# Scores of two levels in one visit of the recurrent branch, larger offsets in the order, and an earlier start of that branch

## The chip, the cores and the metric

The kernel runs on one core of one Trainium2 chip. The metric is the device time of one execution in microseconds (us). Three executions of the kernel before took 2306.87, 2311.93 and 2312.58 us; the median is 2311.93 us.

## What is computed

Two transformer blocks in float32, one after the other, on 512 tokens of width 1024. The change touches the first block alone, apart from one helper that both use. The first block normalizes `x`, projects it, and feeds three branches of 512 columns each, which are merged under gates:

```python
y_a = chunked_relpos_attention(a_q, a_k, a_v, rel_bias[l])      # branch a: attention with a bias by distance
y_b = hgrn2_recurrence(b_q, b_f, b_i, b_g, lb_all[l], ...)      # branch b: the recurrence
y_c = mla_attention(c_q, c_kv, c_kr, positions, ...)            # branch c: latent attention
up = einsum('bsnw,nwd->bsnd', stack([y_a, y_b, y_c]), w_branch[l])
merged = sum(sigmoid(gate_logits) * up, axis=2)
x = x + merged @ w_out[l]
x = x + square(relu(rmsnorm(x) @ w_ff1[l])) @ w_ff2[l]
```

The recurrence of branch b, for each of 8 heads of 64 columns, is

```python
k = (1 - lb) * sigmoid(-z);  q = silu(q)
cum = cumsum(log_f)                       # along the tokens
scores[i, j] = sum_d q[i,d] * k[j,d] * exp(cum[i,d] - cum[j,d])   # j <= i
o = scores @ v                            # plus a state carried from chunk to chunk
o = rmsnorm(o) * silu(g)
```

The second block has two layers, each with two kinds of attention (one of them a retention whose output is normalized per head), a convolutional feed-forward part and a gated addition.

## The kernel before, in words

**Matmuls.** Tiles are feature-major: 128 features by 512 tokens. A float32 product is made as three matmuls of a high and a low part (`lin`, L503: high weight by high x, low weight by high x, high weight by low x), each 128x128 by 512 columns. The weights come from memory in raw tiles of 512 KB, and ScalarE makes the high part (`wh`) and VectorE the low part (`wl`) of each.

**The order.** All instructions of an engine run in the order in which the program issues them, and that order is made by a planner inside the kernel. Every piece of work is a generator (a process) with a priority number. A process yields either nothing, a delay, an event or a condition; `drive` (L301) always continues the ready process with the lowest number. The planner keeps a time of its own, `now`, which only matmuls advance (`mm`, L378, by an estimate for each), and an estimate of when VectorE, ScalarE and GpSimd will have finished what has been issued to them (`Eng`, L211). `self.w("dv")` is the estimated time until VectorE is through, plus 200 ns. So a delay in a `yield` doesn't make any engine wait by itself: it moves what the process issues next behind more matmuls of others. If an estimate is too short, TensorE comes to the instruction before its operand is there, and waits.

**The stream.** One process of the lowest precedence, `stream` (L340), runs a list of tasks one after another: projections of 24 matmuls each (`proj`), the value projection of a branch (`values`, 96 matmuls of `v` into four PSUM banks), and `up` (24 matmuls, two output tiles of a branch's merge). `build` (L905) writes this list. `merge(n, m, ...)` (L1132) is two tasks `gate` and one `up`, so 72 matmuls. `bpair(pr)` is three projections (q, z, g), 72 matmuls, and starts the process `hgrn` of a pair of heads with priority 10 + pr. All of these processes come ahead of the stream wherever they are ready; the stream fills TensorE in between. After branch b's pairs and the merges of branch c come eight `gate` tasks, and then `up(1, m)`, which reads the four outputs of branch b, `yb`.

**One pair of branch b** (`hgrn`, L1254). The decayed scores are made level by level: at level s = 1, 2, 4, ..., 256 a query in the second half of a block of 2s tokens meets keys in its first half. `hlev` (L1352) makes for each level `eq` (ScalarE's exp of the running sum `pre`, then VectorE's product with q in `hmul`) and `ek` (exp of `suf`), and steps `pre` and `suf` to the next level with two VectorE additions. It keeps at most two levels in a list `fifo`. `hgrn` takes the first level of the list when its event has come (400 ns after the estimated end of the product), issues its score matmuls for the two heads into two PSUM banks (`level`, L1400, for s up to 64; inline for s of 128 and 256), and VectorE copies the banks through a mask into the two tiles `dg` (COPY_PREDICATED), or, for the two largest levels, `rsplit` splits them. Levels "0" and 1 go another way: `near` (L1388) transposes a product tile `t` on TensorE and sums it. After the last level come the products with the values (`pv`), the output `y`, and its norm (`gnorm`, L1201): squares, transposes (`gs`), a power and a broadcast on GpSimd (`rt`, `ex`), and transposes back (`pb`), after `yield self.w("gp")`. The split of the product is `yb[pr]`. `gnorm` is also used by the eight pairs of retention heads of the second block.

**Counters.** PSUM has eight banks, counted by `live["ps"]`; besides that each use has a limit of its own (`take`): score banks `sc` at most 3, projections `lin` at most 5, `po` 1. Two pairs of branch b can be under way at once.

Of the kernel before, what the change touches and what calls it, by code (L numbers as in the profile page):

```python
# [40 lines left out]
NT = S // 128  # L41
# [206 lines left out]
class Net:  # L248
# [656 lines left out]
    def build(self):  # L905
        I = self.I
        self.lincap = 5
        self.endp = None
        self.N = N = Norm()
        self.spawn(self.load_x(N), 1)  # L910
        self.spawn(self.rstd(N), 1)
        self.macc = [None] * KT
        self.gl = {}
        self.mx = [X() for _ in range(KT)]
        ya, yb, yc = ([X() for _ in range(4)] for _ in range(3))
        C = self.branch_c(N, yc)
        self.branch_a(N, ya, C)
        if self.stop == "a":
            return self.dump(ya)
        C.pair(0)  # L920
        self.gates(0, TUNE["GA"] + TUNE["GB"], N)
        C.pair(1)
        self.gates(0, TUNE["GA"] + TUNE["GB"] + TUNE["GC"], N)
        self.merge(0, 0, ya, N)
        C.pair(2)
        self.merge(0, 2, ya, N)
        C.pair(3)
        self.merge(0, 4, ya, N)
        self.merge(0, 6, ya, N)
        if self.stop == "c":  # L930
            return self.dump(yc)
        bpair = self.branch_b(N, yb)
        bpair(0)
        self.merge(2, 0, yc, N)
        bpair(1)
        self.merge(2, 2, yc, N)
        bpair(2)
        bpair(3)
        self.merge(2, 4, yc, N)
        self.merge(2, 6, yc, N)  # L940
        gs = [X() for _ in range(KT)]
        for m in range(KT):
            self.gate(1, m, N, gs[m])
        self.call(lambda: self.nfree(N))
        if self.stop == "b":
            return self.dump(yb)
        for m in range(0, KT, 2):
            self.up(1, m, yb, gs[m:m + 2], last=True)
        self.call(lambda: self.free(N.rb))
        self.x = [None] * KT  # L950
        N2 = Norm()
        self.wout1(N2)
        if self.stop == "mix":
            return self.dump(self.x)
        self.ffn1(N2)
# [245 lines left out]
    def gnorm(self, o, eps):  # L1201

        nc = self.nc
        sq = yield from self.g("sq")
        self.ac.activation(sq, o, AF.Square)
        yield self.w("ac")
        ps = yield from self.psr("po", 1, "gs")
        sums = yield from self.rowsum(ps, sq, HD)
        self.free(sq)
        ms = self.powm(sums, 2 * NT, 1.0 / HD, eps)  # L1210
        yield next(ms)
        self.free(ps)
        rt = yield from ms
        ex = yield from self.g("ex")
        self.pl.tensor_scalar(out=ex.rearrange("p (a b) -> p a b", b=64),
                                in0=rt.rearrange("p (a b) -> p a b", b=1).to_broadcast([128, 2 * NT, 64]),
                                scalar1=1.0, scalar2=1.0, op0=ALU.mult, op1=ALU.mult)
        yield self.w("gp")
        pb = yield from self.psr("po", 1, "pb")
        for t in range(NT):  # L1220
            s = slice(128 * t, 128 * t + 128)
            self.tr(pb[:, s], ex[:, s])
        self.free(ex)
        yield 300.0
        return pb
# [28 lines left out]
    def hgrn(self, pr, q, z, gz, vs, y):  # L1254
        nc = self.nc
# [17 lines left out]
        dg = []  # L1273
        for e in range(2):
            d = yield from self.g("dg")
            self.pl.memset(d, 0.0)
            dg.append(d)
        hi, lo = [], []
        fifo = []
        self.spawn(self.hlev(q, pre, suf, fifo), 1)  # L1280
        done = [Ev() for _ in range(2)]
        t = yield from self.g("t0")
        self.dv.tensor_tensor(out=t, in0=q, in1=k, op=ALU.mult)
        yield from self.near(t, 7, dg)
        cnt = [[0], [0]]
        s = 1
        while s < S:
            yield lambda: len(fifo) > 0
            eq, ek, ev = fifo[0]
            yield ev  # L1290
            if s == 1:
                t = yield from self.g("t1")
                self.pl.memset(t, 0.0)
                yield self.w("gp")
                tk, qq, kk = (x.rearrange("p (b u) -> p b u", u=2) for x in (t, eq, k))
                self.dv.tensor_tensor(out=tk[:, :, 0], in0=qq[:, :, 1], in1=kk[:, :, 0], op=ALU.mult)
                yield from self.near(t, 6, dg)
            elif s <= 64:
                yield from self.level(eq, ek, 6 - s.bit_length() + 1, dg)
                if s == 64:  # L1300
                    yield from self.take("Bt", 1, 1)
                    for e in range(2):
                        hi.append((yield from self.tri("sh", F32R)))
                        lo.append((yield from self.tri("sl", F32R)))
                    for e in range(2):
                        self.spawn(self.dsplit(dg[e], hi[e], lo[e], cnt[e], done[e]), 0)
            else:
                for e in range(2):
                    r = slice(64 * e, 64 * e + 64)
                    ps = yield from self.psr("sc", 3, "sc")  # L1310
                    if s == 128:
                        for c in range(2):
                            a, b = slice(256 * c, 256 * c + 128), slice(256 * c + 128, 256 * c + 256)
                            self.mm(ps[:, 128 * c:128 * c + 128], ek[r, a], eq[r, b], True, True)
                        arg = (128, 896, 128)
                    else:
                        for c in range(2):
                            self.mm(ps[:, 256 * c:256 * c + 256], ek[r, 128 * c:128 * c + 128], eq[r, 256:512], True, True)
                        arg = (256, 384, 256)
                    self.spawn(self.rsplit(ps, hi[e], lo[e], arg, cnt[e], done[e]), 0)  # L1320
                    yield None
            fifo.pop(0)
            self.free(eq)
            if s > 1:
                self.free(ek)
            s *= 2
        self.free(q, k, pre, suf)
        self.give("Bl")
        yv = yield from self.g("y")
# [52 lines left out]
    def hmul(self, q, eq, ev):  # L1382
        self.dv.tensor_tensor(out=eq, in0=q, in1=eq, op=ALU.mult)
        self.sig(ev, "dv", "ac")
        ev.t += 400.0
        yield None

    def near(self, t, n, dg):  # L1388

        yield self.w("dv")  # L1390
        ps = yield from self.psr("sc", 3, "sc")
        d = yield from self.rowsum(ps, t, HD)
        self.free(ps, t)
        yield self.w("dv")
        m = self.lev[:, 128 * n:128 * n + 128].rearrange("p (c j) -> p c j", c=1).to_broadcast([128, NT, 128])
        for e in range(2):
            self.dv.copy_predicated(dg[e].rearrange("p (c j) -> p c j", c=NT), m,
                                      d.rearrange("p (t e) -> p t e", e=2)[:, :, e:e + 1].to_broadcast([128, NT, 128]))

    def level(self, qt, kt, n, dg):  # L1400

        nc = self.nc
        pss = []
        for e in range(2):
            pss.append((yield from self.psr("sc", 3, "sc")))
        if n == 0:
            for c in range(NT):
                for e in range(2):
                    r = slice(64 * e, 64 * e + 64)
                    self.mm(pss[e][0:64, 64 * c:64 * c + 64], kt[r, 128 * c:128 * c + 64], qt[r, 128 * c + 64:128 * c + 128], True, True)  # L1410
            for e in range(2):
                self.dv.tensor_copy(dg[e][0:64].rearrange("p (c j) -> p c j", c=NT)[:, :, 64:128],
                                    pss[e][0:64, 0:256].rearrange("p (c j) -> p c j", c=NT))
                self.free(pss[e])
            yield None
            return
        for c in range(NT):
            a = slice(128 * c, 128 * c + 128)
            for e in range(2):
                r = slice(64 * e, 64 * e + 64)  # L1420
                self.mm(pss[e][:, a], kt[r, a], qt[r, a], True, True)
        m = self.lev[:, 128 * n:128 * n + 128].rearrange("p (c j) -> p c j", c=1).to_broadcast([128, NT, 128])
        for e in range(2):
            self.dv.copy_predicated(dg[e].rearrange("p (c j) -> p c j", c=NT), m,
                                      pss[e].rearrange("p (c j) -> p c j", c=NT))
            self.free(pss[e])
        yield None

    def dsplit(self, dg, hi, lo, cnt, done):
        nc = self.nc  # L1430
# [783 lines left out]
```

## Time and profile before

| | |
|---|---|
| three executions | 2306.87, 2311.93, 2312.58 us; median 2311.93 us |
| the profiled execution | 2311.08 us, of which its span is 2309.3 us |
| busy in the span | PE 2274.6 us, PEld 1866.0 us, DVE 1505.5 us, ACT 1094.1 us, POOL 382.4 us |
| granted clock, mean of the span | 0.996 |
| memory | 228.24 MB in DMA packets, 99 GB/s |

PE is TensorE's matmuls, PEld its weight loads, DVE is VectorE, ACT is ScalarE, POOL is GpSimd. Matmuls overlap in the pipeline, so a busy share of PE near all of the span says that something is always in flight, not how fast matmuls follow each other; that is read from the distance between the starts of two of them. A float32 matmul on 64 rows stands in the trace as two records, so that the eight score matmuls of a level are sixteen records. Tiles go by the program's names without numbers: `sc<-eq,ek` are the score matmuls of branch b, `lin` those of the stream.

### The profile page before, as it was taken

To read this page: it belongs to the slowest core of one execution; us is meant where nothing else is said; L and a number is where in the kernel's file an instruction comes from. 1 tells how busy PE (TensorE), PEld (TensorE's weight loads), DVE (VectorE), ACT (ScalarE), POOL (GpSimd) and SP (SyncE) were. 2 spreads that over 40 slices of the span, in tenths; PEclk is the share of its full clock that TensorE was granted. 3 is DMA by queue.
4 is the path that set the end of the run, shared out by engine and by line. 5 is a ranking of instruction groups with operands and counts; after the bars stand their busy time and mean duration, and the time that the engine had idled before them with its cause. 6 is when DMAs were issued, how large, how long until landed. Compare 5 with 4: busy or idle time off the path is not lost.

```text
span 2309.3 us, 28932 instructions
## 1 busy us (share of the span) xinstructions
PE 2274.6 (98%) x10810; PEld 1866.0 (81%) x10810; DVE 1505.5 (65%) x2379; ACT 1094.1 (47%) x1760; POOL 382.4 (17%) x471
## 2 busy tenths in 40 slices
PE   9999999999999999999999999999999999999998
PEld 6887877778888888888778888888888878888886
DVE  6878489975642554679966652457679966652566
ACT  4767476663322333467644331245567644331343
POOL 3523022211000002313320000002312420000012
PEclk9999999999999999999999999999999999999999
DMA  5321222123232232533332223323433333233331
GB/s 179 87 74 56 91 74 64 65 87 123 92 100 99 94 101 76 161 98 95 121 111 92 99 93 101 104 88 114 135 101 106 107 108 101 93 100 100 101 100 65
DMA packets 75726, 228.24 MB, mean 99 GB/s; under 512 B 9664, under 2 KB 15680, under 8 KB 75584
## 3 DMA queue, kind: packets, MB, share of 16 engines
q1 hardware_dynamic: 70400, 209.62, 28.0%
q0 software_dynamic: 5184, 16.75, 2.4%
q8 instruction: 85, 1.39, 0.3%
q14 instruction: 57, 0.47, 0.1%
HBM read 215.29 MB, written 6.32 MB: 96 GB/s over the span
## 4 chain that ended last, share of the span: by engine, by line
PE 87%; DVE 8%; issue 2%; DMA 1%; ACT 1%; POOL 0%; SPq 0%; DVEq 0%; POOLq 0%; ACTq 0%
PE lin L379 74%; PE v L379 5%; PE sc L379 3%; PE po L379 2%; DVE wl L221 2%; PE pt L389 1%; DVE xl L221 1%; DVE dg L221 1%; DVE pl L221 1%; DVE st L221 1%; DMA rb<-ra 0%; DVE ra L221 0%; DVE ql L221 0%; DVE qk L221 0%; DVE ks L221 0%
## 5 line engine op out<-in xcount | busy, mean ns | idle before, releaser
L379 PE MATMUL lin<-xh,wh 128*128 128x512 f32 (+1 forms) x2752 | 1086.9, 395 | 0.2
L379 PE MATMUL lin<-xl,wh 128*128 128x512 f32 (+1 forms) x2752 | 1071.5, 389 | 6.7 <-DVE xl L221 6.7
L379 PE MATMUL lin<-xh,wl 128*128 128x512 f32 (+1 forms) x2728 | 1060.8, 389 | 0.0
L221 DVE TENSOR_TENSOR wl<-raw,wh 128x1024 fp32r<-128x1024 f32 (+3 forms) x391 | 459.7, 1176 | 503.7 <-PE lin L379 326.2
L221 ACT ACTIVATE wh<-raw 128x1024 fp32r<-128x1024 f32 (+4 forms) x394 | 392.3, 996 | 808.3 <-PE lin L379 659.9
L379 PEld LDWEIGHTS lin<-xl,wh 128*128 128x128 f32 x2752 | 516.7, 188 | 118.1 <-DVE xl L221 8.8
L379 PEld LDWEIGHTS lin<-xh,wh 128*128 128x128 f32 x2752 | 517.3, 188 | 105.1 <-issue 3.5
L379 PEld LDWEIGHTS lin<-xh,wl 128*128 128x128 f32 x2728 | 513.8, 188 | 96.3
L221 POOL TENSOR_TENSOR sq<-sq 128x512 f32<-128x512 f32 (+1 forms) x61 | 90.1, 1477 | 570.3 <-ACT sq L221 569.6
L221 POOL MEMSET pad<- 128x2 f32 x44 | 4.4, 99 | 587.7 <-DVE cv L221 587.7
L221 DVE SCALAR_TENSOR_TENSOR cv<-pad,vec,cv 128x512 f32<-128x512 f32 x88 | 66.1, 752 | 40.7 <-ACT cv L221 39.0
L379 PE MATMUL v<-wl,xh 128*128 128x512 f32 x192 | 76.0, 396 | 2.9 <-DVE wl L221 2.9
L379 PE MATMUL v<-wh,xh 128*128 128x512 f32 x192 | 78.0, 406 | 0.6 <-POOL wh L221 0.6
L379 PE MATMUL v<-wh,xl 128*128 128x512 f32 x192 | 75.7, 394 | 0.0
L221 ACT ACTIVATE ph<-pt 128x512 fp32r<-128x512 f32 (+3 forms) x128 | 55.3, 432 | 38.8 <-PE pt L389 38.0
L221 DVE TENSOR_TENSOR x<-lin,x 128x512 f32<-128x512 f32 x80 | 54.7, 684 | 23.4 <-PE lin L379 23.4
L221 ACT ACT_TABLE_LOAD x52 | 66.7, 1283 | 4.4 <-DVE gate L221 2.3
L221 DVE CUSTOM_DVE_ANT_0 lg<-sc,E 128x128 f32<-128x128 f32 (+1 forms) x96 | 45.8, 485 | 31.9 <-PE sc L379 26.1
L221 DVE TENSOR_TENSOR pl<-pt,ph 128x512 fp32r<-128x512 f32 (+3 forms) x128 | 60.2, 479 | 8.2 <-ACT ph L221 7.6
L221 ACT ACTIVATE P<-lg,m 128x128 f32<-128x128 f32 (+1 forms) x96 | 53.3, 556 | 21.6 <-DVE m L221 19.8
L379 PE MATMUL po<-ph,vs 128*128 128x512 f32 x192 | 62.3, 329 | 0.7 <-DVE q L221 0.7
L379 PE MATMUL po<-pl,vs 128*128 128x512 f32 x192 | 60.2, 328 | 2.4 <-DVE pl L221 2.0
(244 smaller groups left out, 2507.8 us busy)
## 6 DMA issues: line engine op xcount, KB each, us to landing
raw<-wup SPq DMA_DIRECT2D x88, 512.0 KB, 3.3
raw<-w SPq DMA_DIRECT2D x83, 512.0 KB, 3.6
raw<-wf SPq DMA_DIRECT2D x64, 512.0 KB, 3.3
raw<-wdn SPq DMA_DIRECT2D x32, 512.0 KB, 3.5
raw<-wv SPq DMA_DIRECT2D x22, 512.0 KB, 3.5
raw<-wpg SPq DMA_DIRECT2D x16, 512.0 KB, 3.3
raw<-wbr SPq DMA_DIRECT2D x12, 512.0 KB, 3.3
raw<-wdn SPq DMA_DIRECT2D x16, 384.0 KB, 3.1
```

What stands on the lines that cost most here:

```text
L221: r = f(*a, **k)
L379: self.nc.tensor.matmul(out, l, r, start=start, stop=stop)
L389: self.nc.tensor.transpose(out, src, self.ident)
```

## The change

- The visits for the levels from 2 up are made in twos: 2 with 4, 8 with 16, 32 with 64, 128 with 256. `hgrn` waits until two levels are in the list and for the event of the second, takes four score banks (limit raised from 3 to 4), issues all score matmuls of both levels in one piece (`level`, and the inline code), frees the operands, and then issues the masked copies (`keep`, new) or splits of both.
- Three offsets of the order are larger: the event of a level comes 700 instead of 400 ns after the estimate (`hmul`), the transposes of `near` 600 ns later, the transposes back in `gnorm` 1500 ns later.
- In `build` the values of branch b and the projections of its first pair come ahead of `merge(0, 6)`, the last merge of the first branch, and no longer behind it.

The number of score matmuls, copies, exponentials and weight loads stays as it was.

```diff
         C.pair(3)
         self.merge(0, 4, ya, N)
+        bpair = self.branch_b(N, yb)
+        bpair(0)
         self.merge(0, 6, ya, N)
         if self.stop == "c":
             return self.dump(yc)
-        bpair = self.branch_b(N, yb)
-        bpair(0)
         self.merge(2, 0, yc, N)
...
-        yield self.w("gp")
+        yield self.w("gp") + 1500.0
         pb = yield from self.psr("po", 1, "pb")
...
+            yield lambda: len(fifo) > 1
+            yield fifo[1][2]
+            yield from self.take("sc", 4, 4)
+            pss = []
+            for _ in range(4):
+                t = yield from self.ps("sc")
+                self.tags[id(t)] = ("ps:sc", t)
+                pss.append(t)
+            for half in range(2):
+                eq, ek, ev = fifo.pop(0)
+                p2 = pss[2 * half:2 * half + 2]
+                if s <= 64:
+                    self.level(eq, ek, 7 - s.bit_length(), p2)
+                else:
+                    for e in range(2):
+                        r, ps = slice(64 * e, 64 * e + 64), p2[e]
...
+                self.free(eq, ek)
+                s *= 2
+            for half in range(2):
+                n, p2 = s >> (2 - half), pss[2 * half:2 * half + 2]
+                if n <= 64:
+                    self.keep(7 - n.bit_length(), p2, dg)
+                else:
+                    arg = (128, 896, 128) if n == 128 else (256, 384, 256)
+                    for e in range(2):
+                        self.spawn(self.rsplit(p2[e], hi[e], lo[e], arg, cnt[e], done[e]), 0)
+                if n == 64:
                     yield from self.take("Bt", 1, 1)
...
         self.sig(ev, "dv", "ac")
-        ev.t += 400.0
+        ev.t += 700.0
...
     def near(self, t, n, dg):
 
-        yield self.w("dv")
+        yield self.w("dv") + 600.0
...
+    def keep(self, n, pss, dg):
+
         m = self.lev[:, 128 * n:128 * n + 128].rearrange("p (c j) -> p c j", c=1).to_broadcast([128, NT, 128])
         for e in range(2):
-            self.dv.copy_predicated(dg[e].rearrange("p (c j) -> p c j", c=NT), m,
-                                      pss[e].rearrange("p (c j) -> p c j", c=NT))
+            d = dg[e].rearrange("p (c j) -> p c j", c=NT)
+            if n == 0:
+                self.dv.tensor_copy(d[0:64, :, 64:128], pss[e][0:64, 0:256].rearrange("p (c j) -> p c j", c=NT))
+            else:
+                self.dv.copy_predicated(d, m, pss[e].rearrange("p (c j) -> p c j", c=NT))
             self.free(pss[e])
```

## Rows read from the trace of the kernel before

**Rows 1.** Busy time of each engine over the span (page, part 1).

```profile
PE 2274.6 (98%) x10810; PEld 1866.0 (81%) x10810; DVE 1505.5 (65%) x2379; ACT 1094.1 (47%) x1760; POOL 382.4 (17%) x471
```

**Rows 2.** Waits of PE, 297 to 515 us: us in total, times, longest us.

```profile
PE pb L389 <- POOL ex L221: 4.4, 2, 2.3
PE sc L389 <- DVE t L221: 1.2, 1, 1.2
PE sc L379 <- DVE eq L221: 1.1, 4, 0.3
...
```

**Rows 3.** Busy time by stretch: us, PE, PEld, DVE, ACT, POOL, clock, DMA share, GB/s.

```profile
251.00:273.00 22.00, 22.00 (x99) 18.22 (x98) 5.53 (x6) 4.26 (x4) 0.00 (x0) 1.00 0.29 95
...
297.00:515.00 218.00, 210.64 (x1252) 166.44 (x1251) 191.92 (x312) 149.15 (x210) 44.81 (x38) 1.00 0.23 72
```

**Rows 4.** PE in order of time round one level's visit: start us, length us.

```profile
306.09 0.39 PE L379 MATMUL lin<-xh,wl 128*128 128x512 f32 x1
306.32 0.40 PE L379 MATMUL lin<-xl,wh 128*128 128x512 f32 x1
306.64 1.16 PE L379 MATMUL sc<-eq,ek 64*128 64x128 f32 x16
307.74 0.50 PE L379 MATMUL lin<-xh,wh 128*128 128x512 f32 x1
308.07 0.40 PE L379 MATMUL lin<-xh,wl 128*128 128x512 f32 x1
```

**Rows 5.** The same view: the visit of level 128, with half as many records.

```profile
335.45 0.72 PE L379 MATMUL sc<-eq,ek 64*128 64x128 f32 x8
336.10 0.50 PE L379 MATMUL lin<-xh,wh 128*128 128x512 f32 x1
```

**Rows 6.** PE by form, 297 to 500 us: count, busy us, mean ns, idle before.

```profile
L379 PE MATMUL sc<-eq,ek 64*128 64x128 f32 x352 | 26.1, 285 | 0.6 <-DVE eq L221 0.4
...
L379 PE MATMUL sc<-eq,ek 64*128 64x256 f32 x32 | 4.7, 401 | 0.3 <-DVE eq L221 0.3
...
L379 PE MATMUL sc<-eq,ek 64*64 64x64 f32 x64 | 2.7, 224 | 0.3 <-DVE eq L221 0.3
```

**Rows 7.** PE in order of time: last visit of pair 2, first and last of pair 3.

```profile
441.58 1.28 PE L379 MATMUL sc<-eq,ek 64*128 64x256 f32 x8
...
454.19 1.16 PE L379 MATMUL sc<-eq,ek 64*128 64x128 f32 x16
...
491.55 1.14 PE L379 MATMUL sc<-eq,ek 64*128 64x256 f32 x8
```

**Rows 8.** VectorE by line and tile, 297 to 515 us: count, busy us, mean ns.

```profile
L221 DVE COPY_PREDICATED dg<-lev,sc 128x512 f32<-128x512 uint8 x40 | 27.0, 730 | 4.3 <-PE sc L379 4.1
L221 DVE TENSOR_TENSOR eq<-qk,eq 128x512 f32<-128x512 f32 x36 | 26.5, 737 | 0.0
L221 DVE TENSOR_TENSOR pre<-pre 128x256 f32<-128x256 f32 x32 | 16.0, 499 | 1.8 <-ACT eq L221 0.5
L221 DVE TENSOR_TENSOR suf<-suf,pre 128x256 f32<-128x256 f32 x32 | 14.2, 444 | 0.7 <-ACT ek L221 0.6
```

**Rows 9.** Instructions on tile eq: ScalarE's exp, ns min/median/max.

```profile
L221 ACT ACTIVATE eq<-pre x36: 608/632/638, 297.3 to 486.3; 128x512 f32<-128x512 f32 x36
```

**Rows 10.** VectorE in order of time: the last split of branch b's last pair.

```profile
513.88 0.68 DVE L221 TENSOR_TENSOR xl<-qk,xh 128x512 fp32r<-128x512 f32 x1
```

**Rows 11.** PE in order of time: the matmul that reads that split.

```profile
514.61 0.50 PE L379 MATMUL lin<-xl,wh 128*128 128x512 f32 x1
```

**Rows 12.** VectorE in order of time: last split of a retention layer's last pair.

```profile
1168.18 0.69 DVE L221 TENSOR_TENSOR xl<-qk,xh 128x512 fp32r<-128x512 f32 x1
```

**Rows 13.** PE in order of time: two waits at a later norm.

```profile
1201.05 0.50 PE L379 MATMUL lin<-xl,wh 128*128 128x512 f32 x1 [0.90 <-DVE xl L221]
...
1204.45 0.79 PE L379 MATMUL lin<-xl,wh 128*128 128x512 f32 x1 [2.42 <-DVE xl L221]
```

**Rows 14.** Busy time and granted clock behind these waits, columns as in rows 3.

```profile
1204.50:1207.70 3.20, 3.20 (x8) 2.42 (x9) 2.11 (x4) 0.00 (x0) 0.00 (x0) 0.50 0.30 122
```

## What I expect, and why

> **What bounds the kernel.** I read the page's busy times first, then who PE waited for, then the stretches, and last PE in order of time. PE is busy for 2274.6 of 2309.3 us [rows 1], so only what PE does, or what it waits for, can change the time. The distance of starts says more than the share: in the stream a 512-column matmul starts 0.23 us after the one before (306.09 to 306.32) [rows 4], and this goes on for nearly all of the span. So the change can win in two ways alone: less PE time around the same score matmuls, and fewer waits. The stretch that it touches is 297 to 515 us, where branch b runs. There PE waits 4.4 us for the broadcast `ex` in two waits, 1.2 us for `t` and 1.1 us for `eq` [rows 2]. VectorE is busy for 191.9 of the 218 us of that stretch, 88%, and ScalarE for 149.2 [rows 3]: branch b moves at VectorE's pace, and PE has the stream to fill in.
>
> **Visits in twos.** From the stream's last matmul before a visit to the second one behind it pass 1.75 us (306.32 to 308.07) [rows 4]. Without the visit it would be two steps of 0.23, 0.46 us, so a visit of sixteen records costs 1.29 us. How much of that is fixed shows beside the visit of level 128: eight records, and 0.65 us from its start to the next stream matmul (335.45 to 336.10) [rows 5], where sixteen take 1.10 (306.64 to 307.74) [rows 4]. Eight records more cost 0.45 us, 0.056 each. So eight are worth 0.45 and 0.20 us of the visit is fixed; to this come the late entry (0.32 for 0.23, so 0.09) and the late second step behind it (0.33 for 0.23, so 0.10): 0.39 us for each visit. Two levels in one piece should take 1.29 + 16 x 0.056 = 2.19 us where two visits take 2.58.
>
> The count: 352 records of 64x128 are 20 levels of sixteen and 4 of eight, to which come 4 visits of 64-column and 4 of 256-column records [rows 6], 32 visits in all, eight for each pair of heads. Sixteen go: 16 x 0.39 = 6.2 us. All of them lie on PE, which nothing hides. The least that I can defend is the two late steps alone, 16 x 0.19 = 3.0 us, if the 0.20 inside a visit doesn't go; the most is 6.4. I take 6.2, because both visits have the same shape and alternate between two halves of the rows, as a double one will.
>
> A rule speaks against it. The Trainium skill, in "TensorE: Matmul & The Clock Gate", section "Back-to-back issue gap", gives about 81 ns for a 128-column matmul in a sustained stream with its weight loads. By that the second sixteen would cost 1.30 us, as much as a visit of its own, and the sum would be 0 for this part. The trace shows 56 ns a record between eight and sixteen, so I go by the trace.
>
> **Waits.** The transposes back in `gnorm` wait 2.3 us at most and 4.4 in two [rows 2]; the order put them there before GpSimd was through. 1500 ns more in the order takes 1.5 off each: 3.0 us (bounds 0 and 4.4). The wait for `t`, 1.2 us, loses 0.6 of it (0 to 1.2). The four waits for `eq` are at most 0.3 us long [rows 2], and the event is now 300 ns later and half as often waited for: 1.0 of 1.1 (0 to 1.1). Together 4.6 us, from 0 to 6.7. All these places are filled with stream matmuls instead, which are there to the end of the branch.
>
> **What is added.** The visit now waits for the second level's `eq` and for four banks; queued behind it on PE is the stream, and behind the four masked copies on VectorE (0.73 us each [rows 8], so 2.9 in one piece instead of 1.5) the next weight parts `wl` and gate evacuations. The weight parts are made up to three tiles ahead, that is over 10 us of matmuls, so 1.5 us later hides. Four score banks leave four for all else, which the stream seldom needs at once. The rows don't show this case. From below, nothing; from above, the waits that now stand in the stretch come again in other places, 6.7 us. I take 1.0, nearer to nothing, because the order still issues the reads of a bank before it hands it out.
>
> **What is moved.** The values (96 matmuls, four weight tiles) and the first three projections (72 matmuls, three tiles) go ahead of 72 matmuls of `merge(0, 6)`. Their weight loads on SP's queue, and the splits on ScalarE and VectorE, move in the same order as the matmuls, three tiles ahead, so no queue gets more. GpSimd gets nothing new: `merge(0, ...)` adds nothing up. The values now meet the last heads of branch c; while they run, VectorE is busy for 5.5 of 22 us [rows 3], so there is room. The eight tiles of `ya` live 168 x 0.227 = 38 us longer, which can hold back a gate's evacuation in one PSUM bank; five are allowed. Price: nothing, or, if the cover fails, one gate's evacuation of a few us. By itself the move gains nothing, since PE does the same work. It starts branch b 72 x 0.227 = 16.3 us earlier against the stream.
>
> **Where that is needed.** The last split of `yb` ends at 514.56 us [rows 10], and the matmul that reads it starts at 514.61 [rows 11]. So today branch b ends just as the stream needs it: anything that shortens PE's work makes the end of branch b the next thing to be late. PE's need moves forward by 6.2 + 4.6 - 1.0 = 9.8 us. Branch b's end moves forward by 16.3 less 1.5 (`gnorm`) less 1.2 (two `near` of the last pair) = 13.6 us, less what the visits in twos add to a pair's chain. That leaves 3.8 us. For two levels a pair now takes 10.7 us (37.4 us from first to last visit, over seven steps, times two) [rows 7]. In series two levels need exp 0.63 and two additions 0.94, twice, one product 0.74 [rows 8, 9], the offset of 0.9, and the visit of 2.2: 7.0 us. So a double step can be 3.7 us shorter, or, if the visit comes on top of today's pace because `hlev` can't run ahead during it, 2.2 us longer. VectorE gets no new work, so I take 0.5 longer. The first pairs have room (12.6 us lie between pair 2's last visit and pair 3's first [rows 7]), so the last two pairs count, eight visits: 4 us, 0.2 more than there is. With what the estimate hides I charge 0.8 us.
>
> **The helper elsewhere.** `gnorm` also serves eight pairs of retention heads. The last split of the first layer's last pair ends at 1168.2 us [rows 12], and the first wait of PE behind it is at 1201.1, for another tile [rows 13]: 1.5 us later is hidden. Price 0; without the cover 1.5 us for each of two layers.
>
> **Sum.** -6.2 - 4.6 + 1.0 + 0.8 = -9.0 us. The profiled execution took 2311.1 us, 0.8 below the median of the three, so I take **2302 us**.
>
> **Rivals.** First, the end of branch b is late. If each double visit adds 1.5 us to the chain, eight add 12 where 3.8 is free: PE waits 8 us before `up(1, ...)`, and 2 us are left of the gain, 2309 us. Against it: no VectorE work is added. For it: there is no slack today [rows 10, 11].
>
> Second, the same and slower than before. It decides at 8 x - 3.8 = 9.8 + 6.9, x = 2.6 us a double visit, above the bound of 2.2. But a wait of this length also costs clock: behind two waits of 0.9 and 2.4 us [rows 13] the granted clock was 0.50 for 3.2 us, the level of 1.2 GHz [rows 14], which loses 1.6 us. With that, x of 2.4 is enough; at 3 us, PE waits 20 us, loses 1.6 to the clock, and the time is 2311 - 10 + 22 = 2323 us. This needs a visit that VectorE and ScalarE don't use for anything else.
>
> Third, the waits come back. The gains at `pb`, `t` and `eq` return at other places as the order shifts: 2311 - 6.2 + about 2 = 2307 us.
>
> Fourth, a longer run of score matmuls is no cheaper. If records in the second half of a double visit cost 0.081 us, twice a visit is what it costs, and only the waits are left: 2311 - 4.6 + 1.8 = 2308 us. Eight against sixteen records [rows 4, 5] speak against it. The rule of the skill above would make it so.
>
> Fifth, more than forecast. All of the stall bounds and no new wait: 6.4 + 6.7 = 13.1, 2298 us or a little less.
>
> **Chances.** Forecast, 2298 to 2305: 0.53. More than forecast: 0.07. Late end of branch b, 2305 to 2317: 0.19. Waits come back: 0.10. No cheaper: 0.04. Slower: 0.07. About 0.3% (7 us) is what a measurement of this kernel can tell from no change: faster means under 2305.0, slower over 2318.9. Faster 0.53 + 0.07 = 0.60, slower 0.07, within 0.33. For eight in ten the range takes the forecast, half of "more", the returned waits and the no-cheaper case, and two thirds of the late end: 2296 to 2312 us, 0.83.
>
> **What would show it.** Right: sixteen visits `sc<-eq,ek` of 32 records, 2.0 us from start to the next stream matmul (1.99 by 1.10 + 16 x 0.056); waits for `ex` under 1 us each; the first score visit some 16 us earlier; the reader of the last `yb` without a wait over 1 us. Wrong: 2.4 us for a double visit (no cheaper); a wait `lin <- xl` of several us before the first `up(1, ...)`, with granted clock below 1 behind it (late end); waits of PE on banks, for masked copies or gate evacuations, that sum to over 3 us (waits come back).

## The result, and the profile after

The changed kernel took 2324.49 us (median of six, 2323.38 to 2325.88), the kernel before in the same job 2311.35 us: ratio 1.0054, 95% interval 1.0045 to 1.0064. It is slower by 0.54%, where I had 9 us faster. What came is the second rival: branch b's end is late. The busy times of the page, to be read against [rows 1], say nothing of it: PE's is the same, and only the span is longer (2323.0 us for 2309.3). ScalarE's seven instructions more are loads of its function tables (59 for 52, 1.28 us each).

```profile
PE 2273.7 (98%) x10810; PEld 1871.9 (81%) x10810; DVE 1508.1 (65%) x2379; ACT 1102.9 (47%) x1767; POOL 383.1 (16%) x471
```

A double visit of two levels of sixteen records costs what was computed. PE in order of time, beside [rows 4]: 32 records, 1.99 us from their start (301.08) to the next stream matmul (303.07), where I had 1.99.

```profile
301.08 2.06 PE L379 MATMUL sc<-eq,ek 64*128 64x128 f32 x32
303.07 0.50 PE L379 MATMUL lin<-xh,wh 128*128 128x512 f32 x1
```

The stretches, columns as in [rows 3], show gain and loss one behind the other:

```profile
297.00:492.60 195.60, 195.58 (x1172) 160.52 (x1170) 171.80 (x270) 137.45 (x185) 41.39 (x32) 1.00 0.25 76
492.60:521.80 29.20, 12.45 (x73) 9.37 (x72) 14.83 (x30) 13.99 (x23) 5.61 (x6) 0.63 0.10 31
521.80:530.00 8.20, 8.18 (x25) 6.49 (x26) 4.20 (x6) 1.70 (x2) 0.00 (x0) 0.67 0.16 51
```

To 492.6 us PE never stops: the waits of [rows 2] are gone there. Then the stream has nothing left that doesn't read `yb`, and PE works alone on the last pair's remaining levels, values and norm, 12.45 busy us in 29.2. PE in order of time, with the wait before each in brackets:

```profile
492.25 0.39 PE L379 MATMUL lin<-xl,wh 128*128 128x512 f32 x1
495.33 1.16 PE L379 MATMUL sc<-eq,ek 64*128 64x128 f32 x16 [2.69 <-DVE eq L221]
498.77 1.12 PE L379 MATMUL sc<-eq,ek 64*64 64x64 f32 x16 [2.28 <-DVE eq L221]
502.17 1.23 PE L379 MATMUL sc<-eq,ek 64*128 64x128 f32 x8 [2.29 <-ACT eq L221]
...
514.24 1.12 PE L389 MATMUL gs<-cst,sq 128*128 128x128 f32 x4 [3.14 <-ACT sq L221]
519.21 1.12 PE L389 MATMUL pb<-cst,ex 128*128 128x128 f32 x4 [3.85 <-POOL ex L221]
521.82 0.79 PE L379 MATMUL lin<-xh,wh 128*128 128x512 f32 x1 [1.50 <-ACT xh L221]
...
522.84 0.63 PE L379 MATMUL lin<-xl,wh 128*128 128x512 f32 x1
```

The last line is the matmul of [rows 11], at 514.61 us before. The sum, roughly: PE stands 29.2 - 12.45 = 16.8 us; at the mean clocks above, the low clock loses 12.45 x 0.37 = 4.6 there and 8.2 x 0.33 = 2.7 behind it; the visits give back 5.2 (worked out in the section on the prediction) and the old waits 218 - 210.64 = 7.4 [rows 3]. That makes +11.5; matched stream matmul by stream matmul, the profiled execution of after loses 9.8 us between 300 and 530 us. The 1.7 us between the two stay open; a mean clock over a stretch that is mostly waiting is a coarse measure. Another 3.0 us are lost where the second block's retention heads are.

Why the end is late shows in the starts of the score visits (us; the first and last of each pair):

| pair | 0 | 1 | 2 | 3 |
|---|---|---|---|---|
| before | 306.6 to 339.5 | 355.8 to 393.0 | 408.4 to 441.6 | 454.2 to 491.6 |
| after | 301.1 to 340.8 | 364.5 to 402.8 | 406.7 to 449.9 | 475.5 to 503.8 |

Pairs 0 to 2 take 13.5 us for a double step (121.2 us over nine) where two levels took 9.8 before (103.3 us over 21 steps, times two): 3.6 us longer. And the first visit is only 5.5 us earlier, though the first `near` is 14.4 earlier (283.0 for 297.4).

That pair 3 starts 21 us later comes from pair 1. Only two pairs may be under way, so the first instruction of pair 3 (`f`, on ScalarE) follows the transposes back of pair 1's norm (`pb`, on PE). First before, then after:

```profile
414.54 0.66 PE L389 MATMUL pb<-cst,ex 128*128 128x128 f32 x4
415.83 0.62 ACT L221 ACTIVATE f<-qk 128x512 f32<-128x512 f32 x1
```

```profile
433.77 0.60 PE L389 MATMUL pb<-cst,ex 128*128 128x128 f32 x4
436.35 0.63 ACT L221 ACTIVATE f<-qk 128x512 f32<-128x512 f32 x1
```

The two stand as close in e4 (414.9 and 416.4) and e7 (410.7 and 411.5), and within 7 us of each other in every kernel but e13 (12.3). No run changes the limit of two, so this link is read from traces alone.

VectorE points to the cause. Its waits for score matmuls ahead of the masked copies, 290 to 492 us (us in total, times, longest), first before, then after:

```profile
DVE dg L221 <- PE sc L379: 6.6, 7, 2.2
```

```profile
DVE dg L221 <- PE sc L379: 12.3, 7, 3.4
```

One of them in order of time, in after:

```profile
326.59 1.77 PE L379 MATMUL sc<-eq,ek 64*128 64x128 f32 x32
...
327.78 1.35 DVE L221 COPY_PREDICATED dg<-lev,sc 128x512 f32<-128x512 uint8 x2 [2.85 <-PE sc L379]
```

The sum varies between executions: e10, with the same program as before in this stretch, has 9.7 us. Over all sixteen kernels it is 3.6 to 9.7 us where a level can be made ahead of the visit, and 10.9 to 20.0 us in the six where none can (after, e2, e5, e9, e14, and e8 in its first pair).

The copies stand in VectorE's order, and PE's scores are there 2.85 us after VectorE is ready for them. In that time VectorE could work on the pair's next levels; but `fifo` holds two, both places belong to the visit that is due, and `hlev` may not go on. Then both places come free at once, and the next two levels are made one after the other behind the copies.

### The profile page after: what moved, and what is told of

It is laid out like the page before. It is cut to its first block, busy times and chain, and to the rows that moved or that the text cites. A ratio compares the mean times of both kernels' runs of the same rounds, so it can differ in the third digit from the quotient of the medians.

```text
span 2323.0 us, 28933 instructions
## 1 busy us (share of the span) xinstructions
PE 2273.7 (98%) x10810; PEld 1871.9 (81%) x10810; DVE 1508.1 (65%) x2379; ACT 1102.9 (47%) x1767; POOL 383.1 (16%) x471
## 4 chain that ended last, share of the span: by engine, by line
PE 92%; DVE 4%; issue 1%; ACT 1%; DMA 1%; POOL 0%; SPq 0%; DVEq 0%; POOLq 0%; ACTq 0%
PE lin L379 78%; PE v L379 5%; PE sc L379 4%; PE po L379 3%; PE pt L389 1%; DVE wl L221 1%; DVE xl L221 1%; DVE ks L221 0%; DVE ql L221 0%; DMA rb<-ra 0%; DVE st L221 0%; DMA w<-wv 0%; DVE pl L221 0%; PE cs L389 0%; DVE ra L221 0%
```

## The experiments

Each kernel was compared with the kernel before on the same chip; that one's median was 2312.05 to 2312.27 us in all four jobs. "Reader" is the matmul of [rows 11]. No kernel leaves work out.

**Which part does it.** Three parts, each put back or done alone.

e1: offsets and move, visits of one level.

```diff
-            yield lambda: len(fifo) > 1
-            yield fifo[1][2]
-            yield from self.take("sc", 4, 4)
...
+            elif s <= 64:
+                yield from self.level(eq, ek, 6 - s.bit_length() + 1, dg)
...
```

> The changed kernel with one part undone: the visits are made level by level again; the larger offsets and the earlier start stay. Theory A (waiting for two levels with a list of two stretches each pair's chain, so that branch b ends some 20 us after the stream has run dry): the end is in time again, the 22 us of the tail go, the sixteen fixed parts of 0.39 us come back; with the waits for ex, t and eq gone but 3 us lost in the retention layers 2306 to 2311 us. Theory B (the larger offsets stretch the chain): the tail stays, 2318 us or more. Theory C (the earlier start puts the first pair into branch c and holds tiles): 2318 us or more too.

Measured 2316.63 us, ratio 1.0020 (1.0011 to 1.0030). The reader starts at 516.4 us, 1.8 later than in before, though the split that it reads is through at 510.9: branch b's end is in time again, and the stream itself is late. The time lies above the range of theory A; waits came back in the middle, 5.8 us, at other places than before (`eq` 3.7).

e2: double visits and move, offsets as before (400, 0, 0).

> The changed kernel with the three offsets as before (400 ns, 0, 0); visits in twos and earlier start stay. Theory A: the tail is only 3 to 5 us shorter, the 3 us in the retention layers go, waits for ex come back: 2316 to 2323 us. Theory B: the tail goes, and the visits' 6 us are won: 2303 to 2308 us. Theory C: as the changed kernel less 3, 2321 us.

Measured 2321.17 us, 1.0039 (1.0024 to 1.0054). The tail is the same, reader at 522.9; the loss in the second block is gone.

e3: the offsets alone, on the kernel before.

> The kernel before with the larger offsets alone. Theory A: waits for ex, t and eq shrink by some 5 us, branch b ends a few us later where it had no room, and the retention layers lose 3 us: 2309 to 2315 us. Theory B: the chain is longer by 1.5 + 1.2 us and more for each pair, and the end is late by over 8 us: 2318 us or more. Theory C says nothing against 2309 to 2315 us.

Measured 2313.21 us, 1.0003 (0.9994 to 1.0012). The waits for `ex` are gone (4.4 to 0), and the time isn't shorter: `eq` is waited for 3.6 us instead of 1.1, and branch b still ends when the reader needs it (split through at 513.98, reader 514.04). By stream matmuls 0.2 us are won between 300 and 530 us, and 3.0 are lost in the second block.

e4: the move alone, on the kernel before.

> The kernel before with the earlier start alone. Theory A: PE does the same work, branch b ends some 10 us before it is needed, waits as before: 2308 to 2313 us. Theory B: the same. Theory C: the first pair's matmuls meet branch c's, gates wait for tiles, 2316 us or more.

Measured 2306.73 us, 0.9978 (0.9969 to 0.9988): faster than before, and than each of the theories had it. The reader starts at 508.75 us with the split through at 508.7, and the waits of PE in the stretch of [rows 2] fall to 3.4 us. So the move holds nothing back, the offsets alone don't make the tail, and double visits cost 14.4 us beside the move (e2 against e4). The parts don't simply add up: the offsets cost about 1 us alone and 9.9 us beside the move with single visits (e1 against e4).

**Is it the visit or the list?** e5 has no double visit. It takes e4 and lets the list hold one level instead of two, so that none is made ahead of the one that is due:

```diff
-            while len(fifo) > 1:
-                yield lambda: len(fifo) < 2
+            while len(fifo) > 0:
+                yield lambda: len(fifo) < 1
```

> Only the move of the first pair and the values, score visits one level each as before, old offsets, and the list of levels made ahead (`fifo`) holds one level where the kernel before holds two. No double visits are left. Theory A (after is slow because two levels that must leave a list of two together stop `hlev` from making levels ahead of the visits, so that a pair's levels come in series): the same happens here with single visits. The step for two levels grows from 9.4 to 10.7 us to about 13, the reader of the last `yb` starts near 520 to 523 us where only the move has 508.8, and the time is 2318 to 2325 us. Rival D (the double visit itself, its four banks or its length on the PE, stretches the chain): nothing of that is here, so the step stays near 10 us and the time near that of only the move, 2307 us (2304 to 2310).

Measured 2330.90 us, 1.0080 (1.0065 to 1.0095), past the upper end. The first pair's two levels take 13.8 us (299.0 to 347.2 over seven steps), the reader starts at 532.1, and the tail has the shape of after's. PE's waits, 297 to 533 us, and VectorE's for the scores, 290 to 492:

```profile
PE sc L379 <- DVE eq L221: 9.2, 5, 2.8
PE pb L389 <- POOL ex L221: 3.9, 1, 3.9
PE gs L389 <- ACT sq L221: 3.1, 1, 3.1
...
```

```profile
DVE dg L221 <- PE sc L379: 20.0, 15, 2.8
```

So single visits without a level made ahead are slower still, and long visits and four banks aren't needed for the late end.

e6: the same as e4 with a list of three.

> Only the move, single visits, old offsets, and the list of levels made ahead holds three. Theory A: run-ahead is what sets a pair's pace, so one place more makes the steps somewhat shorter or leaves them, the end of branch b is on time (reader of the last `yb` at 509 us or a little earlier, no wait there), and the waits for eq (1.8 us with only the move) fall under 1 us: 2303 to 2307 us. Rival E (VectorE's own work sets the pace, the list does not matter): 2307 us, as only the move. Rival F (tiles of the pool run short with one level more, and weight parts come later): waits of PE on weight parts or gate evacuations of some us, 2308 to 2312.

Measured 2308.49 us, 0.9985 (0.9975 to 0.9994), no gain over e4, and the waits for `eq` are 4.9 us, not under 1. One level ahead is enough for visits of one; rival E comes nearest. The time fits rival F too, but its waits, on weight parts or gates, aren't there.

e7: double visits, move, old offsets, list of three. The tiles for the third place come from a lower reserve (gates and projections leave 4 tiles free, not 8).

```diff
-    MARGIN=8,
+    MARGIN=4,
...
-            while len(fifo) > 1:
-                yield lambda: len(fifo) < 2
+            while len(fifo) > 2:
+                yield lambda: len(fifo) < 3
```

> Double visits and the move, old offsets, with a list of three levels; the third place is paid for by a lower reserve in the pool (MARGIN 4 for 8, tiles that gates and projections leave free). Theory A: part of the run-ahead is back, the third level is made while the first two wait, so a double step falls from 13.2 us to 11 to 12, the wait ahead of the first up(1, ...) is about halved, and the time is 2310 to 2317 us where double visits with the list of two and old offsets took 2321. Rival D (the double visit itself is slow): 2319 to 2323 us.

Measured 2307.41 us, 0.9978 (0.9969 to 0.9988): 13.8 us less than e2, more than I gave it. The first visit stands at 294.5 us (300.5 in e2), the double steps take 10.9 us (130.6 us over all twelve; in pairs 0 to 2 of e2 13.4), the reader starts at 508.2, and VectorE waits less than half as long for the scores:

```profile
DVE dg L221 <- PE sc L379: 5.7, 6, 1.8
```

e7 has four banks, long visits and 62 loads of ScalarE's tables (59 in after), so none of these makes the end late by itself. What is left of the tail are the last pair's norm and its split (PE in order of time):

```profile
504.33 1.11 PE L389 MATMUL pb<-cst,ex 128*128 128x128 f32 x4 [3.85 <-POOL ex L221]
507.22 0.80 PE L379 MATMUL lin<-xh,wh 128*128 128x512 f32 x1 [1.78 <-ACT xh L221]
```

e9: the control for e7, with the lower reserve and the list of two.

> Control for the run with double visits and a list of three: double visits, the move, old offsets, list of TWO, and the lower reserve of the pool (4 for 8). If the place in the list did the work there, this stays where double visits with the list of two were: reader of the last `yb` at 521 to 524 us, 2319 to 2323 us. If the lower reserve did it, this is near 2307 us with the reader near 508.

Measured 2318.41 us, 1.0029 (1.0020 to 1.0039), a little under the range. Reader at 522.1, VectorE's wait for the scores 14.1 us in seven (14.6 in eight in e2). Of the 13.8 us between e2 and e7 the reserve accounts for 2.8 at face value, and the intervals of e9 and e2 overlap; the place in the list does the rest.

e8: double visits in the first pair only (`two = s < 256 and pr < 1`), the rest as e4.

> Double visits in the first of branch b's four pairs only, single visits in the other three; the move, old offsets, list of two. Four visits less than with only the move: 4 x 0.39 = 1.6 us of PE. Theory A with room at the front (the first pair's delay is taken up by later pairs): the end of branch b is 0 to 4 us later than with only the move (reader at 508.8 us), so the time is 2305 to 2311 us, centre 2308. If the delay is not taken up at all, the first pair's growth of 4 steps x 3 us = 12 us goes through to the end: reader near 520 us, 2317 to 2320 us.

Measured 2307.75 us, 0.9979 (0.9970 to 0.9988). The first pair ends at 340.8 us for 323.0, the last pair's first visit stands at 454.8 for 451.0, the reader at 511.2 for 508.75: of 18 us of delay 2.5 are left at the end. So there is room between pairs for one slow pair; for more than one, after is the case.

**Can the gain be had?** e11 takes e7 and asks for the pairs earlier:

```diff
         self.merge(0, 4, ya, N)
         bpair = self.branch_b(N, yb)
         bpair(0)
         self.merge(0, 6, ya, N)
-        self.merge(2, 0, yc, N)
         bpair(1)
+        self.merge(2, 0, yc, N)
+        bpair(2)
         self.merge(2, 2, yc, N)
-        bpair(2)
         bpair(3)
```

> Double visits with a list of three (reserve 4), the move, old offsets, and the pairs asked for earlier: pair 1 ahead of merge(2, 0), pair 2 behind it, pair 3 behind merge(2, 2). Theory A: what was left to wait for with the list of three was the end of the last pair (8.4 us of waits, ex 3.9, sq 2.1, xh 1.8); 16 to 20 us more of stream lie behind the last pair's projections now, so these waits go and the 6.2 us of the visits show: PE waits in branch b 1 to 3 us, the stream 9 to 11 us ahead of the kernel before behind branch b, 2300 to 2304 us, ratio 0.995 to 0.9965. Rival D2 (pairs share VectorE and the bank of the transposes, so asking earlier doesn't make the last one earlier): reader near 508 us as before, 2306 to 2308 us.

Measured 2297.01 us (2295.59 to 2297.68), 0.9933 (0.9919 to 0.9947), under the range and the fastest kernel of the study, 15 us less than before. PE's waits in the whole stretch of [rows 2], and then the last split (VectorE) and its reader (PE) in order of time:

```profile
PE po L379 <- DVE sl L221: 0.7, 1, 0.7
PE sc L389 <- DVE t L221: 0.5, 1, 0.5
PE sc L379 <- DVE sl L221: 0.3, 1, 0.3
```

```profile
501.33 0.68 DVE L221 TENSOR_TENSOR xl<-qk,xh 128x512 fp32r<-128x512 f32 x1
```

```profile
501.68 0.39 PE L379 MATMUL lin<-xh,wl 128*128 128x512 f32 x1
502.07 0.50 PE L379 MATMUL lin<-xl,wh 128*128 128x512 f32 x1
```

Branch b still ends just as the stream needs it, with the split through at 502.01 and the reader at 502.07, but the reader, 0.39 us behind the matmul before it where a step is 0.23, loses no more than 0.2 us.

e13 takes the double visits out of it, and e14 the third place of the list with the reserve that pays for it. e13: single visits, list, reserve and order as e11.

> The order of e11 (pairs asked for earlier), list of three, reserve 4, but single visits. Against e11 this undoes the double visits alone. If a visit's fixed 0.39 us is real and nothing else bounds branch b any more, this is 6.2 us slower than e11: 2302 to 2305 us, with at most 3 us of PE waits in branch b. Rival: the gain of e11 over only the move came from the order alone, and this is 2296 to 2299 us.

Measured 2310.77 us, 0.9993 (0.9984 to 1.0002): 13.8 us more than e11, and more than I gave it. In the profiled executions (e13's is the slowest of its eleven, 4.7 us over the median) e13 loses 13.2 us on e11 in branch b. Of these, 8.0 are waits, 9.5 for 1.5 us, most for `eq`, for which e11 never waits:

```profile
PE sc L379 <- DVE eq L221: 5.7, 8, 1.4
PE sc L379 <- ACT eq L221: 2.4, 4, 0.9
...
```

The other 5.2 us fit what sixteen visits less are worth (6.2 in the prediction). Branch b's end isn't what holds e13 up: its split is through at 495.05, 21.7 us ahead of the reader. Why single visits wait for `eq` in this order wasn't tested.

e14: double visits and the order of e11, list of two, reserve 8.

> The order of e11 with double visits, but the list of two and the reserve 8. If the run-ahead is what the double visit needs, the steps are 13 us long as in after, the first visit stands near 300 us for 295, and the end of branch b is late in spite of the earlier asking: waits of 8 to 16 us ahead of the first up(1, ...), 2308 to 2317 us. Rival: asking earlier is enough, the list doesn't matter, 2297 to 2301 us.

Measured 2314.74 us, 1.0011 (1.0002 to 1.0020), as expected. The tail is back, though the pairs are asked for earlier (PE's waits, 297 to 525 us, the longest lines):

```profile
PE pb L389 <- POOL ex L221: 3.9, 1, 3.9
PE sc L389 <- DVE t L221: 2.9, 2, 1.7
...
```

**The norm's offset.** e10 is the kernel before with the 1500 ns in the second block alone:

```diff
-        yield self.w("gp")
+        yield self.w("gp") + (1500.0 if eps == GN_EPS else 0.0)
```

> The kernel before with one edit: the 1500 ns after the broadcast `ex` in `gnorm` for the eight retention pairs of the second block alone, nothing in branch b. Theory G (the later transposes back there make the next retention heads later, which PE waits for): nothing changes up to 515 us, the stream is 2.3 to 3 us later behind the two stretches of retention, and the time is 2314 to 2316 us, ratio 1.001 to 1.0013. Rival (the 3 us of the kernels with offsets came from the shift of the other offsets or of the first block): 2311 to 2313 us.

Measured 2316.78 us, 1.0018 (1.0009 to 1.0026), just over theory G's range. PE's waits from 1090 to 1150 us, before and e10; the wait for `st` is new:

```profile
PE po L379 <- DVE pl L221: 1.4, 3, 0.6
PE sc L379 <- DVE m L221: 1.2, 1, 1.2
```

```profile
PE po L379 <- DVE pl L221: 2.7, 3, 1.1
PE sc L379 <- DVE m L221: 1.5, 1, 1.5
PE sc L379 <- DVE st L221: 1.4, 1, 1.4
```

By stream matmuls the two retention stretches lose 2.4 and 1.4 us. e12 is e11 with the 1500 ns in branch b alone.

> As the run with the pairs asked for earlier, with 1500 ns behind the broadcast `ex` in branch b's four pairs alone (not in retention). If the waits for ex are still there without it (0.5 to 4 us), they go and the time is 1 to 3 us lower than that run's; if they went with the order already, it is the same or, by the last pair's later end, 0 to 2 us higher. Range 2298 to 2306 us.

Measured 2299.77 us, 0.9947 (0.9935 to 0.9960). e11 has no wait for `ex` left to remove; in e12 the last pair's output comes 1.5 us late for PE (`lin` for `xh`). The offset buys nothing there either; whether it costs the 2.8 us between the medians is not settled, as the two intervals overlap.

## Why the prediction was wrong

**Right.** The visit of 32 records of 64x128, as eight of the sixteen are: 1.99 us computed, 1.99 measured. So the rule of the Trainium skill, "TensorE: Matmul & The Clock Gate", section "Back-to-back issue gap", that the prediction weighed and put aside (81 ns a matmul) doesn't hold for these records: sixteen more take 1.99 - 1.10 = 0.89 us, 56 ns each. The waits of [rows 2] went up to 492.6 us, and the move cost nothing (e4); that anything which shortens PE's work makes the end of branch b late next was right, and is the result.

**The step that failed** is the chain, under "Where that is needed": "a double step can be 3.7 us shorter, or ... 2.2 us longer", of which I took 0.5. It is 3.6 longer, and what it adds reaches the last pair from all the pairs ahead of it. Three things were wrong in it.

- The upper bound charged a stop of `hlev` with the visit alone. What stops is more: VectorE stands at the copies until PE comes (2.85 us in the row shown), makes four copies, and then both levels in series, with the stream's weight parts and gates between. The lower bound, 7.0 us in series, counted none of that on an engine that is 88% busy [rows 3], nor the second exp of each level, `ek`. e5 shows that the run-ahead is enough to explain the pace: taken from single visits, two levels of the first pair take 13.8 us there. How the 3.6 us divide among these parts isn't measured.
- "The first pairs have room, so the last two pairs count." They have (e8 gives back 15 of 18 us), but not for three pairs in a row: after pair 1's end at 402.8 us pair 2 starts at 406.7, where 15.4 us lay between them before, and pair 3 starts 21 us later than before, behind pair 1's norm. With two pairs under way at most, pair 1's delay is pair 3's.
- "Branch b's end moves forward by 13.6 us." The first visit moved 5.5. It waits for levels 2 and 4 now, and level 4 can't enter the list before level 1 has left it. e7, with one place more, has it at 294.5.

The second rival had the late end but not its size: it decides at 2.4 us a double visit, and at 3 it gave 2323. Its chance of 0.07 hung on the bound of 2.2. That 2323 lies so near 2324.5 is in part luck: it has 20 us of waits for 16.8, 1.6 for the clock where some 7 were lost, and nothing for `gnorm`.

**"By itself the move gains nothing"** was wrong too: e4 is 5.5 us faster than before. In its profiled execution the waits for `ex` are 0.6 us for 4.4, with no offset changed: where branch b starts earlier, other matmuls stand between the broadcast and the transposes. Why the order leaves them just there I didn't test.

**Mis-sized.** The visits: 6.2 us for sixteen at 0.39 each, "because both visits have the same shape". Half of them don't have it. PE in order of time, first the visit of level 64 in before, then in after the first stream matmul behind the visit of 32 and 64 (it starts at 326.59, shown above), and the visit of 128 and 256:

```profile
330.53 0.68 PE L379 MATMUL sc<-eq,ek 64*64 64x64 f32 x16
331.14 0.50 PE L379 MATMUL lin<-xh,wh 128*128 128x512 f32 x1
```

```profile
328.29 0.50 PE L379 MATMUL lin<-xh,wh 128*128 128x512 f32 x1
...
340.75 1.68 PE L379 MATMUL sc<-eq,ek 64*128 64x128 f32 x16
342.37 0.50 PE L379 MATMUL lin<-xh,wh 128*128 128x512 f32 x1
```

From start to next stream matmul 32 and 64 take 1.10 and 0.61 us alone and 1.70 together; 128 and 256 take 0.65 [rows 5] and 1.07 (491.55 [rows 7] to 492.62) alone and 1.62 together. So inside a visit 0.21, 0.21, 0.01 and 0.10 us go, and with the late steps of 0.19 each a pair saves 1.29 us and four pairs 5.2. e13 against e11 left 5.2 too.

The clock: 1.6 us for a long wait, about 7 by the rough sum above, because the tail isn't one wait but eight with slow matmuls between. And `gnorm` elsewhere: "1.5 us later is hidden. Price 0", measured 3.0 us in after's profiled execution and 4.7 between the medians of e10 and before (2 to 6 by the interval). I looked for cover of the last pair's split alone; e10's waits are at other places, at the scores and values of the heads that follow in the order.

**The forecast of the waits** (4.6 us gone) came true in after up to 492.6 us only; behind that come 16.8 us of others. e3 has the offsets without the move: the `ex` waits go, others come, no gain. That was the third rival.

## What to carry to other kernels

Before two visits are made one, count the places ahead of them: a batch that takes all of a queue's places at once takes the run-ahead too, and the maker stands while it is drained. Here single visits had enough with a list of two (a third place gained nothing, e6), and double ones needed three. Where a chain ends just in time, a gain on the engine that consumes it is only to be had together with an earlier end of the chain: the doubled visits were worth -14 us with room (e11 against e13; 5 of them PE's own time, 8 waits) and +14 without (e2 against e4). And where a limit lets two chains run at a time, ask which earlier chain the last one has to wait for.

## What the runs showed of the hardware

The clock behind a short wait isn't the same in each execution. Up to 515 us e10 has the program of before, and both wait 2.3 us for `ex` at the same place. First before, then e10: the wait (PE in order of time), and a stretch of 2 us behind it (columns as in [rows 3]).

```profile
362.21 0.66 PE L389 MATMUL pb<-cst,ex 128*128 128x128 f32 x4 [2.30 <-POOL ex L221]
```

```profile
364.00:366.00 2.00, 2.00 (x21) 1.61 (x20) 1.97 (x5) 1.60 (x3) 0.00 (x0) 1.00 0.00 0
```

```profile
360.60 0.67 PE L389 MATMUL pb<-cst,ex 128*128 128x128 f32 x4 [2.33 <-POOL ex L221]
```

```profile
362.00:364.00 2.00, 2.00 (x7) 1.16 (x7) 1.90 (x4) 1.21 (x3) 0.00 (x0) 0.50 0.00 0
```

In before the granted clock is 1.00 behind it, the level of 2.4 GHz (and 1.00 from 362 us on), in e10 it is 0.50, the level of 1.2 GHz. The same happens at the second such wait, near 466 us, and e10's execution loses 1.6 and 1.5 us on before's at these two places. So a wait of 2.3 us cost 2.3 us in one and about 3.9 in the other. Of the 7 us between the fastest and the slowest execution of before (2306.87 and 2313.72) this can be a part; that isn't shown.
